# Seven-product pairs in the down projection: 30 of 44 instead of 24, with activation sums kept in DRAM and weights tiled by the host

## The chip, the cores and the metric

The kernel runs on one core of one Trainium2 chip. The metric is the device time of one execution, in microseconds; the median of several runs is given. TensorE (PE) multiplies, PEld is its weight load, VectorE (DVE), ScalarE (ACT) and GpSimd (POOL) do the elementwise work, and SyncE (SP) issues nearly all transfers.

## The reference

The input is one sequence of 256 tokens with 2048 features, in float32. What is computed, cut to what matters here:

```python
hn  = rmsnorm(h, mix_norm_pre);  proj = hn @ w_in            # 2048 x 3616
mix = concat(ssd_mixer(z, xbc, dt), pool_mixer(u)) @ w_out   # 2048 x 2048
h   = h + rmsnorm(mix, mix_norm_post)
hn  = rmsnorm(h, ffn_norm_pre)
up  = hn @ w_ffn_up                                          # 2048 x 11264
gate, val = split(up)                                        # 5632 each
gate = dwconv_centred(gate, conv_w, conv_b)                  # three taps over tokens
h   = h + rmsnorm((gelu(gate) * val) @ w_ffn_down, ffn_norm_post)  # 5632 x 2048
g   = sigmoid(rmsnorm(h, ple_norm_pre) @ w_ple_gate)         # 2048 x 2048
h   = h + rmsnorm(g * (p @ w_ple), ple_norm_post)
```

## The kernel before

**Precision.** Every float32 operand of a large product is split into a high part (a rounded copy by ScalarE) and a low part (the rest, a subtraction by VectorE). A product of two operands then takes three matmuls: high by high, high by low, low by high. For weights, `split` does this (L141 to L153: the copy on L152, the subtraction on L153); the parts lie in tiles of the tags `whi` and `wlo`, with five buffers each. All matmuls go through the helper `mm` on L87.

**Stages, in order.** The input projection and the mixers, w_out, then the gated MLP in two stages: "up" (11 slices of 512 features, first the gate columns, then the value columns) and "down" (two halves of 1024 output columns). Last come the gate of the per-layer embedding (also two halves) and the output. The names of tiles begin with `ug` and `uv` in up, `dn0` and `dn1` in the two halves of down, `gt0` and `gt1` in the gate, and `wo` in w_out.

**Pairs.** `token_major` (L291) walks a half in pairs: two blocks of 128 input features by 1024 columns of weights, loaded as one tile of the tag `raw` (three buffers, L156). Down has 22 pairs a half and the gate 8. A plain pair takes 24 matmuls of 512 columns.

**Seven products.** `seven_products` (L239) does a pair by Strassen's scheme: the two blocks of 128 rows and the two of 512 columns form a 2 x 2 block product, made with seven block products instead of eight, 21 matmuls. It needs sums of the four weight blocks (`add_blocks`, L235 to L237: one addition of 1024 columns and two of 512) and sums of the four activation blocks (`pair_sums`, L774: four small additions, L777 to L780, then the split in high and low on L781 and L782). The weights come as four split tiles: `a` (512 columns), `b`, `c` and `d` (1024 each); `c` and `d` are made of the sums. `combine` (L269) adds the seven results at the end of a half's last such pair. Pairs treated so are called fast.

**Where the sums come from.** If a pair is listed in `sums_`, its weight sums were made during up and the pair loads them (`t`) beside 0.75 MB of its weights; else the pair loads its 1 MB and `add_blocks` runs in place. The w_out stage works in the second way, as its pair `wo10` shows. Before, all 24 fast pairs of down (12 a half) and the 4 of the gate have their weight sums made during up: `block_sums` (L208) loads a pair, adds, and stores the result in DRAM (two stay on chip). These jobs lie in a list, `work`, of 88 entries; `aside` (L196) runs one entry behind each of the 88 units of up. The activation sums are made in down itself by `hid_sums` (L920): 20 times, as four of the first half's are kept on chip for the second (`dn_keep`).

**Activations in down.** `get_hid` (L899) splits two blocks of the hidden activations into one tile of the tag `hs` (two buffers; the copy on L903, the subtraction on L904). Small tiles of 1024 columns share the tag `mid` (three buffers).

**Order.** Each engine works through its own queue in program order; a scheduler puts the instructions into these queues ahead of time. `load` (L119) issues transfers on SP. `first_gate` (L943) is called at pair 16 of the second half: it prepares the first pair of the gate by two casts on ScalarE (L948, L950) and one accumulating transfer issued by GpSimd (L949). `back`, at pair 13, loads the residual again.

Of the kernel before, what the change touches and what calls it, by code (L numbers as in the profile page):

```python
# [16 lines left out]
P = 128  # L17
L = 256
# [33 lines left out]
def build(nc, a, out):  # L52
    x = a["x"][0]
    w_in, w_out, w_up = a["w_in"][0], a["w_out"][0], a["w_ffn_up"][0]
    w_down, w_gate, w_ple = a["w_ffn_down"][0], a["w_ple_gate"][0], a["w_ple"][0]
    out = out[0]

    with tile.TileContext(nc) as tc, \
# [37 lines left out]
        c_dt = DSSD + 1536  # L96
        r0 = wp.tile([P, 2048], F32, tag="raw", bufs=3, name="dtur0")
        for n in range(2):
            first = ins(nc.scalar.dma_start(r0[:, n * 352:(n + 1) * 352],
                                            w_in[:P, c_dt + n * 352:c_dt + (n + 1) * 352]))  # L100
# [55 lines left out]
        def raw(name, src, a_, b_):  # L156
            r = wp.tile([P, 2048], F32, tag="raw", bufs=3, name=name)
            if src is None:
                return r
            last["dma"] = load(r[:, :a_ * b_].rearrange("p (a b) -> p a b", a=a_), src, True)  # L160
            return r
# [46 lines left out]
        def block_sums(name, w, c0, k, held):  # L208


            pg = []

            def fetch():
                r = page(f"{name}b{c0}_{k}")
                pg.append(r)
                load(r.rearrange("p (k c) -> p k c", k=2),
                     w[k * P:(k + 2) * P, c0:c0 + 1024].rearrange("(k p) c -> p k c", p=P))
# [12 lines left out]
            return [fetch], [], [add], [store]  # L230
# [8 lines left out]
        def seven_products(name, stage, w, k0, c0, a_, acc, alt, start, stop):  # L239

            if (stage, c0, k0) in sums_:
                r = raw(f"{name}r", None, 0, 0)
                last["dma"] = load(r[:, 512:1536], w[(k0 + 1) * P:(k0 + 2) * P, c0:c0 + 1024], True)
                last["dma"] = load(r[:, :512], w[k0 * P:(k0 + 1) * P, c0:c0 + 512], True)
                t, held = sums_[stage, c0, k0]
                if not held:
                    t = page(f"{name}t")
                    last["dma"] = load(t, sums_[stage, c0, k0][0], True)  # L250
                b11 = split(f"{name}a", r[:, :512], 512)
                b2 = split(f"{name}b", r[:, 512:1536], 1024)
            else:
                r = t = raw(f"{name}r", w[k0 * P:(k0 + 2) * P, c0:c0 + 1024]
                            .rearrange("(k p) c -> p k c", p=P), 2, 1024)
# [35 lines left out]
        def token_major(name, w, c0, ks, get, acc, tail=1, fast=(), alt=None, sums=None, at=()):  # L291
# [3 lines left out]
            for u in range(nu):  # L295
# [3 lines left out]
                if u in fast:  # L299
                    if u == fast[0]:  # L300
# [3 lines left out]
                r = None if f"{name}{k0}_0" in ready else raw(f"{name}r{k0}", w[k0 * P:(k0 + 2) * P, c0:c0 + 1024]  # L304
                                                               .rearrange("(k p) c -> p k c", p=P), 2, 1024)
# [17 lines left out]
        def feature_major(name, w, c0, get, acc):  # L323

            for u in range(4):
                r = raw(f"{name}r{u}", w[u * 512:(u + 1) * 512, c0:c0 + 512]
                        .rearrange("(k p) c -> p k c", p=P), 4, 512)
# [12 lines left out]
        def feature_pairs(name, w, c0, get, acc):  # L340


            for u in range(2):
                r = raw(f"{name}r{u}", w[u * 1024:(u + 1) * 1024, c0:c0 + 256]
                        .rearrange("(k p) c -> p k c", p=P), 8, 256)
# [97 lines left out]
        for u in range(0, NK, 2):  # L443
            r = [wp.tile([P, 2048], F32, tag="raw", bufs=3, name=f"dtur{u}") if u else r0, page(f"dtur{u + 1}")]
            for j in range(2):
                k = u + j
                if k == 0:
                    last["dma"] = load(r[0][:, 704:1056], w_in[:P, c_dt + 704:c_dt + 1056])
                    xload(1, 2)
                    x_panel(1, 2)  # L450
                    continue
                for c0, c1 in ((0, 704), (704, 1056)) if k == 1 else ((0, 1056),):
                    last["dma"] = load(r[j][:, c0:c1], w_in[k * P:(k + 1) * P, c_dt + c0:c_dt + c1])
# [29 lines left out]
        with tc.issue_after(half[0]), tc.issue_after(half[1]):  # L483
# [11 lines left out]
            for a_ in range(4):  # L495
# [17 lines left out]
        load(pmat.rearrange("p (g s t) -> p g s t", g=4, s=2),  # L513
             a["pool_matrix"].rearrange("g (s p) t -> p g s t", p=P))
        poolw = page("poolw")
        load(poolw.rearrange("p (g c d) -> p g c d", g=4, c=2),
             a["pool_w"][0].rearrange("g (c p) d -> p g c d", p=P))
# [122 lines left out]
        def xbc(slab):  # L640
            acc = main(f"xbc{slab}")
            feature_major(f"xb{slab}", w_in, DSSD + slab * 512, hn, acc)
# [88 lines left out]
        token_major("z", w_in, 0, list(range(NK)), hn, zacc)  # L731
# [42 lines left out]
        def pair_sums(name, s, o, a11, a21, a12, a22):  # L774

            s1, s2, s3, s4 = (s[:, i * P:(i + 1) * P] for i in range(4))
# [5 lines left out]
            nc.vector.tensor_sub(o[:, 512:], s[:, :512], o[:, :512].bitcast(F32))  # L782
            return {f"s{i + 1}": (o[:, i * P:(i + 1) * P], o[:, 512 + i * P:512 + (i + 1) * P]) for i in range(4)}
# [89 lines left out]
        hid = []  # L873
        for s in range(DFF // 512):
            sc = mid(f"gr{s}")
            for i in range(2):
                ga = main(f"ga{s}{i}")
                feature_pairs(f"ug{s}{i}", w_up, s * 512 + i * 256, hf, ga)
# [8 lines left out]
            for i in range(2):  # L887
                va = main(f"va{s}{i}")
                feature_pairs(f"uv{s}{i}", w_up, DFF + s * 512 + i * 256, hf, va)
# [9 lines left out]
        def get_hid(k):  # L899
            if k % 2 == 0:  # L900
                t = lp.tile([P, 1024], F32R, tag="hs", bufs=2, name=f"hs{k}")
                src = hid[k // 8][:, (k % 8) * L:(k % 8 + 2) * L]
                nc.scalar.copy(t[:, :512], src)  # L903
                nc.vector.tensor_sub(t[:, 512:], src, t[:, :512].bitcast(F32))  # L904
# [13 lines left out]
        keep, kept = [], {}  # L918

        def hid_sums(k):  # L920


            (h1, l1), (h2, l2) = get_hid(k), get_hid(k + 1)
            if k not in kept:
                src = hid[k // 8][:, (k % 8) * L:(k % 8 + 2) * L]
# [17 lines left out]
        def first_gate():  # L943

            r, hi, lo = page("gtf"), page("gtfh", F32R), page("gtfl", F32R)
            src = w_gate[:2 * P, :1024].rearrange("(k p) c -> p k c", p=P)
            last["dma"] = load(r.rearrange("p (k c) -> p k c", k=2), src)
            nc.scalar.activation(lo, r, AF.Copy, scale=-1.0)  # L948
            nc.gpsimd.dma_start(lo.rearrange("p (k c) -> p k c", k=2), src, accum_op=ALU.add)  # L949
# [14 lines left out]
        vg = [page(f"vg{t}") for t in range(2)]  # L964
# [27 lines left out]
        for half in range(2):  # L992
# [12 lines left out]
            for t in range(2):  # L1005
                for n, (o, c0) in enumerate(columns(acc[t])):
# [15 lines left out]
                    else:  # L1022
                        nc.scalar.activation(so, sv, AF.Square, accum_out=q)
                    nc.vector.tensor_mul(vg[t][:, c], v, gple[:, c])
# [5 lines left out]
def laid_out(a):  # L1030

    def cols(*vs):
        return np.concatenate([v.reshape(-1, P).T for v in vs], axis=1)

    return {
        "x_cols": np.concatenate([cols(a["mix_norm_pre"][0]),
# [24 lines left out]
def constants():  # L1061
    return {"pool_matrix": pool_matrix()}
# [16 lines left out]
```

## Time and profile before

| | us |
|---|---|
| median of 3 runs | 1123.02 (1122.94 to 1123.16) |
| the profiled execution | 1123.11 |
| span of its instructions | 1121.3 |
| granted TensorE clock, mean | 0.997 |

| stage | window, us | PE busy | DVE busy | ACT busy |
|---|---|---|---|---|
| up | 311.2 to 789.0 | 477.80 | 386.76 | 240.31 |
| down, first half | 789.0 to 902.5 | 113.50 | 105.23 | 81.65 |
| down, second half | 902.5 to 1016.7 | 114.15 | 104.77 | 84.56 |
| gate, first part | 1016.7 to 1068.0 | 51.30 | 42.96 | 33.73 |

The profile comes from one execution, some 2 us longer than the span because it begins before the first instruction and ends behind the last. A row of a timeline gives start, duration, engine, line of the kernel, operation, and the tiles as output<-inputs; what stands in brackets is how long the engine was idle before it and what ended the wait. Durations of neighbours overlap a little, so a price is best read from start to start.

### The profile page before, as it was taken

To read this page: it belongs to the slowest core of one execution; us is meant where nothing else is said; L and a number is where in the kernel's file an instruction comes from. 1 tells how busy PE (TensorE), PEld (TensorE's weight loads), DVE (VectorE), ACT (ScalarE), POOL (GpSimd) and SP (SyncE) were. 2 spreads that over 40 slices of the span, in tenths; PEclk is the share of its full clock that TensorE was granted. 3 is DMA by queue.
4 is the path that set the end of the run, shared out by engine and by line. 5 is a ranking of instruction groups with operands and counts; after the bars stand their busy time and mean duration, and the time that the engine had idled before them with its cause. 6 is when DMAs were issued, how large, how long until landed. Compare 5 with 4: busy or idle time off the path is not lost.

```text
span 1121.3 us, 15775 instructions
## 1 busy us (share of the span) xinstructions
PE 1109.1 (99%) x5971; PEld 956.4 (85%) x5971; DVE 925.2 (83%) x1275; ACT 663.9 (59%) x927; POOL 76.2 (7%) x86
## 2 busy tenths in 40 slices
PE   9999999999999999999999999999999999999996
PEld 9999987888888888888888888888888888888875
DVE  6569895799898877877877768888899999889795
ACT  6847663555764554554545445445677777786672
POOL 0200004200110100000000000000000000001001
PEclk9999999999999999999999999999999999999998
DMA  9862447456789989989999898996969688995663
GB/s 363 310 207 96 170 161 269 151 188 190 252 308 347 328 300 336 314 289 309 333 330 314 276 330 289 325 304 224 339 185 334 221 286 301 383 318 177 230 235 109
DMA packets 145996, 300.87 MB, mean 268 GB/s; under 512 B 5504, under 2 KB 98560, under 8 KB 137856
## 3 DMA queue, kind: packets, MB, share of 16 engines
q1 hardware_dynamic: 145360, 298.45, 78.6%
q0 software_dynamic: 272, 1.05, 0.5%
q8 instruction: 47, 0.77, 0.3%
q10 hardware_dynamic: 288, 0.36, 0.1%
q14 instruction: 29, 0.24, 0.1%
HBM read 268.38 MB, written 31.46 MB: 267 GB/s over the span
## 4 chain that ended last, share of the span: by engine, by line
PE 96%; ACT 1%; DVE 1%; issue 1%; POOL 1%; POOLq 0%; DVEq 0%; ACTq 0%
PE va L87 22%; PE ga L87 21%; PE dna L87 14%; PE woa L87 7%; PE xbc L87 6%; PE gt L87 5%; PE dtu L87 4%; PE z L87 4%; PE dns L87 3%; PE dn0s L87 1%; PE dn1s L87 1%; PE ple L87 1%; PE pw L87 1%; PE yd L87 0%; PE gts L87 0%
## 5 line engine op out<-in xcount | busy, mean ns | idle before, releaser
L87 PE MATMUL ga<-wox,ug_0h 128*128 128x512 f32 x352 | 125.5, 395 | 0.0
L87 PE MATMUL ga<-wox,ug_1h 128*128 128x512 f32 x352 | 125.1, 394 | 0.0
L87 PE MATMUL va<-wox,uv_1h 128*128 128x512 f32 x352 | 124.8, 393 | 0.0
L87 PE MATMUL va<-wox,uv_0h 128*128 128x512 f32 x352 | 124.8, 393 | 0.0
L87 PE MATMUL ga<-wox,ug_1l 128*128 128x256 f32 x352 | 99.1, 282 | 0.0
L87 PE MATMUL ga<-wox,ug_0l 128*128 128x256 f32 x352 | 99.1, 282 | 0.0
L87 PE MATMUL va<-wox,uv_1l 128*128 128x256 f32 x352 | 99.1, 281 | 0.0
L87 PE MATMUL va<-wox,uv_0l 128*128 128x256 f32 x352 | 99.1, 281 | 0.0
L87 PEld LDWEIGHTS va<-wox,uv_1h 128*128 128x128 f32 x352 | 66.1, 188 | 15.0
L87 PEld LDWEIGHTS va<-wox,uv_0h 128*128 128x128 f32 x352 | 66.1, 188 | 15.0
L87 PEld LDWEIGHTS ga<-wox,ug_0h 128*128 128x128 f32 x352 | 66.1, 188 | 14.9
L87 PEld LDWEIGHTS ga<-wox,ug_1h 128*128 128x128 f32 x352 | 66.1, 188 | 14.9
L87 PEld LDWEIGHTS ga<-wox,ug_0l 128*128 128x128 f32 x352 | 66.2, 188 | 0.1
L87 PEld LDWEIGHTS ga<-wox,ug_1l 128*128 128x128 f32 x352 | 66.2, 188 | 0.0
L87 PEld LDWEIGHTS va<-wox,uv_0l 128*128 128x128 f32 x352 | 66.2, 188 | 0.0
L87 PEld LDWEIGHTS va<-wox,uv_1l 128*128 128x128 f32 x352 | 66.2, 188 | 0.0
L885 POOL TENSOR_TENSOR fc<-fc,rfb 128x1024 f32<-128x1024 f32 x11 | 28.0, 2547 | 438.6 <-ACT fc L884 438.6
L87 PE MATMUL dna<-dn_0h,hs 128*128 128x512 f32 x160 | 50.1, 393 | 0.0
L87 PE MATMUL dna<-dn_1h,hs 128*128 128x512 f32 x160 | 49.9, 393 | 0.0
L235 DVE TENSOR_TENSOR dnb<-dnb 128x1024 f32<-128x1024 f32 x24 | 30.8, 1283 | 17.8 <-DMA dnb<-w_ffn_down 17.6
L903 ACT CAST hs<-hid 128x512 fp32r<-128x512 f32 x44 | 27.2, 617 | 23.2 <-PE dna L87 14.8
L904 DVE TENSOR_TENSOR hs<-hid,hs 128x512 fp32r<-128x512 f32 x44 | 30.2, 686 | 9.8 <-ACT hs L903 9.7
(1903 smaller groups left out, 3105.3 us busy)
## 6 DMA issues: line engine op xcount, KB each, us to landing
dnb<-w_ffn_down SPq DMA_DIRECT2D x24, 1024.0 KB, 10.4
dns<-dnb SPq DMA_DIRECT2D x22, 1024.0 KB, 7.4
dn0r<-w_ffn_down SPq DMA_DIRECT2D x10, 1024.0 KB, 6.0
dn1r<-w_ffn_down SPq DMA_DIRECT2D x10, 1024.0 KB, 7.1
zr<-w_in SPq DMA_DIRECT2D x8, 1024.0 KB, 5.1
dtur<-w_in SPq DMA_DIRECT2D x14, 528.0 KB, 8.7
wo0r<-w_out SPq DMA_DIRECT2D x7, 1024.0 KB, 5.6
wo1r<-w_out SPq DMA_DIRECT2D x6, 1024.0 KB, 5.5
```

The costliest lines, as they stand in the source:

```text
L87: last["pe"] = ins(nc.tensor.matmul(o, lhsT, rhs, start=start, stop=stop, skip_group_check=True))
L235: nc.vector.tensor_add(v[:, 0:2], v[:, 0:2], v[:, 1::2])
L885: nc.gpsimd.tensor_tensor(cv.rearrange("p (f t) -> p f t", f=4), cv.rearrange("p (f t) -> p f t", f=4), rfb.unsqueeze(1).to_broadcast([P, ...
L903: nc.scalar.copy(t[:, :512], src)
L904: nc.vector.tensor_sub(t[:, 512:], src, t[:, :512].bitcast(F32))
```

## The change

- **More fast pairs.** Down goes from 12 and 12 fast pairs to 16 and 14 of 22, the gate from 4 to 5 of 16. The order of the gate's second half is changed to suit.
- **Weight sums.** Eleven of down's 30 fast pairs (`dn_own`) have no weight sums made during up: they run `add_blocks` in place. The other 19 and the gate's 5 are still made during up, spaced 7/2 entries apart instead of 3.
- **Activation sums.** The sums of 16 pairs are made during up, in a tile of the tag `hs`, and stored in DRAM by SP. Down fetches them for each of its 30 fast pairs by a transfer of 512 KB issued by GpSimd, into a `mid` tile.
- **Layout.** The host lays all weights out in tiles, so that each load is contiguous: 8 KB for each partition, where rows of 1 KB (up), 2 KB (xbc) or 4 KB were gathered before.
- The two result pages of the last stage are allocated later.

```diff
-        dn_fast, gt_fast, dn_keep = ((2, 3, 5, 7, 8, 10, 12, 13, 15, 16, 18, 19), (2, 3, 5, 7, 8, 10, 12, 13, 15, 16, 18, 19)), ((4, 6), (1, 2)), (3, 8, 13, 18)
-        gt_ks = list(range(NK)), [0, 1, 12, 13, 8, 9, 2, 3, 4, 5, 6, 7, 10, 11, 14, 15]
-        which = [("dn", w_down, c * 1024, 2 * u) for c in range(2) for u in dn_fast[c]] + \
+        dn_fast, gt_fast = ((2, 3, 4, 5, 6, 8, 9, 10, 11, 12, 14, 15, 16, 17, 18, 19), (2, 3, 4, 5, 8, 9, 10, 11, 12, 14, 15, 17, 18, 19)), ((4, 5, 6), (1, 2))
+        dn_own = (5, 9, 11, 15, 17), (4, 8, 10, 12, 15, 17)
+        gt_ks = list(range(NK)), [0, 1, 8, 9, 10, 11, 2, 3, 4, 5, 6, 7, 12, 13, 14, 15]
+        which = [("dn", w_down, c * 1024, 2 * u) for c in range(2) for u in dn_fast[c] if u not in dn_own[c]] + \
             [("gt", w_gate, c * 1024, gt_ks[c][2 * u]) for c in range(2) for u in gt_fast[c]]
...
-                work[3 * i + 2 + j].extend(jobs)
+                work[7 * i // 2 + 2 + j].extend(jobs)
...
+        def hid_sums_jobs(k):
+            o = []
+            def make():
+                o.append(lp.tile([P, 1024], F32R, tag="hs", bufs=2, name=f"he{k}"))
+                pair_sums(f"he{k}", o[0][:, 512:].bitcast(F32), o[0],
+                          *(hid_part(k)[:, i * P:(i + 1) * P] for i in range(4)))
+            def store():
+                kept[k] = dp.tile([P, 1024], F32, tag=f"hsum{k}", bufs=1, name=f"hsum{k}")
+                load(kept[k], o[0].bitcast(F32))
+            return [make], [store]
+        for u in sorted({*dn_fast[0], *dn_fast[1]}):
+            for j, jobs in enumerate(hid_sums_jobs(2 * u)):
+                work[u // 2 * 8 + u % 2 * 2 + 6 + j].extend(jobs)
...
         def hid_sums(k):
+            o = mid(f"hd{k}", F32R)
+            nc.gpsimd.dma_start(o.bitcast(F32), kept[k])
             (h1, l1), (h2, l2) = get_hid(k), get_hid(k + 1)
-            if k not in kept:
-                src = hid[k // 8][:, (k % 8) * L:(k % 8 + 2) * L]
-                n = dn_keep.index(k // 2) if k // 2 in dn_keep else -1
-                if n >= 0 and n % 2 == 0:
-                    keep.append(page(f"hsum{k}", F32R))
-                o = keep[-1][:, n % 2 * 1024:(n % 2 + 1) * 1024] if n >= 0 else mid(f"he{k}", F32R)
-                d = pair_sums(f"hd{k}", mid(f"hd{k}"), o, *(src[:, i * P:(i + 1) * P] for i in range(4)))
-                if n >= 0:
-                    kept[k] = d
-            else:
-                d = kept[k]
-            return dict(d, a11=(h1[:, :P], l1[:, :P]), a12=(h2[:, :P], l2[:, :P]), a22=(h2[:, P:], l2[:, P:]))
+            return dict(sums_in(o), a11=(h1[:, :P], l1[:, :P]), a12=(h2[:, :P], l2[:, :P]), a22=(h2[:, P:], l2[:, P:]))
...
+    def tiles(w, nk, nc):
+        k, c = w.shape
+        return w.reshape(k // P // nk, nk, P, c // nc, nc).transpose(3, 0, 2, 1, 4).reshape(c // nc, k // P // nk, P, nk * nc)
...
+        "w_up": tiles(a["w_ffn_up"][0], 8, 256).reshape(2, DFF // 512, 2, 2, P, 2048),
+        "w_down": tiles(a["w_ffn_down"][0], 2, 1024),
+        "w_gate": tiles(a["w_ple_gate"][0], 2, 1024),
```

More of the change, by code (lines that the diff above doesn't have):

```diff
@@ L53, in build @@
     x = a["x"][0]
-    w_in, w_out, w_up = a["w_in"][0], a["w_out"][0], a["w_ffn_up"][0]
-    w_down, w_gate, w_ple = a["w_ffn_down"][0], a["w_ple_gate"][0], a["w_ple"][0]
+    w_dtu, w_xbc, w_z, w_out, w_up = a["w_dtu"], a["w_xbc"], a["w_z"], a["w_out_"], a["w_up"]
+    w_down, w_gate, w_ple = a["w_down"], a["w_gate"], a["w_ple_"]
     out = out[0]
@@ L154, in split, with raw @@
             return hi, lo
-        def raw(name, src, a_, b_):
+        def raw(name, src=None):
             r = wp.tile([P, 2048], F32, tag="raw", bufs=3, name=name)
-            if src is None:
-                return r
-            last["dma"] = load(r[:, :a_ * b_].rearrange("p (a b) -> p a b", a=a_), src, True)
+            if src is not None:
+                last["dma"] = load(r, src, True)
             return r
@@ L243, in seven_products @@
             if (stage, c0, k0) in sums_:
-                r = raw(f"{name}r", None, 0, 0)
-                last["dma"] = load(r[:, 512:1536], w[(k0 + 1) * P:(k0 + 2) * P, c0:c0 + 1024], True)
-                last["dma"] = load(r[:, :512], w[k0 * P:(k0 + 1) * P, c0:c0 + 512], True)
+                r = raw(f"{name}r")
+                last["dma"] = load(r[:, 512:1536], w[c0 // 1024, k0 // 2][:, 1024:], True)
+                last["dma"] = load(r[:, :512], w[c0 // 1024, k0 // 2][:, :512], True)
                 t, held = sums_[stage, c0, k0]
@@ L447, in build @@
                 if k == 0:
-                    last["dma"] = load(r[0][:, 704:1056], w_in[:P, c_dt + 704:c_dt + 1056])
+                    last["dma"] = load(r[0][:, 704:1056], w_dtu[0][:, 704:1056])
                     xload(1, 2)
@@ L452, in build @@
                 for c0, c1 in ((0, 704), (704, 1056)) if k == 1 else ((0, 1056),):
-                    last["dma"] = load(r[j][:, c0:c1], w_in[k * P:(k + 1) * P, c_dt + c0:c_dt + c1])
+                    last["dma"] = load(r[j][:, c0:c1], w_dtu[k][:, c0:c1])
                 if k == 1:
@@ L730, in build @@
         zacc = [main(f"z{t}") for t in range(2)]
-        token_major("z", w_in, 0, list(range(NK)), hn, zacc)
+        token_major("z", w_z, 0, list(range(NK)), hn, zacc)
         assert not work
@@ L945, in first_gate @@
             r, hi, lo = page("gtf"), page("gtfh", F32R), page("gtfl", F32R)
-            src = w_gate[:2 * P, :1024].rearrange("(k p) c -> p k c", p=P)
-            last["dma"] = load(r.rearrange("p (k c) -> p k c", k=2), src)
+            last["dma"] = load(r, w_gate[0, 0])
             nc.scalar.activation(lo, r, AF.Copy, scale=-1.0)
-            nc.gpsimd.dma_start(lo.rearrange("p (k c) -> p k c", k=2), src, accum_op=ALU.add)
+            nc.gpsimd.dma_start(lo, w_gate[0, 0], accum_op=ALU.add)
             nc.scalar.copy(hi, r)
@@ L963, in build @@
         gple = gload("gple", a["ple_norm_post"][0])
-        vg = [page(f"vg{t}") for t in range(2)]
+        vg = []
         sq = [[], []]
@@ L1023, in build @@
                         nc.scalar.activation(so, sv, AF.Square, accum_out=q)
+                    if half == n == 0:
+                        vg.append(page(f"vg{t}"))
                     nc.vector.tensor_mul(vg[t][:, c], v, gple[:, c])
@@ L1068 @@
     arrays.update({n: np.ascontiguousarray(v) for n, v in laid_out(arrays).items()})
-    arrays.update(constants())
+    arrays.update({n: np.ascontiguousarray(v) for n, v in constants().items()})
     for n in ("p", "mix_norm_pre", "ssd_conv_w", "ssd_conv_b", "ssd_norm", "pool_scale", "ffn_norm_pre",
-              "ffn_conv_w", "ple_norm_pre", "ffn_conv_b", "ssd_dt_bias", "ssd_a_log", "ssd_d"):
+              "ffn_conv_w", "ple_norm_pre", "ffn_conv_b", "ssd_dt_bias", "ssd_a_log", "ssd_d", "w_in", "w_out",
+              "w_ffn_up", "w_ffn_down", "w_ple_gate", "w_ple", "pool_w"):
         del arrays[n]
```

56 lines of the change are left out of this document (28 added, 28 removed).

## The prediction

> **What bounds the kernel now.** I read the engine table and the shares of the chain of waits first.
>
> ```profile
> PE 1109.1 (99%) x5971; PEld 956.4 (85%) x5971; DVE 925.2 (83%) x1275; ACT 663.9 (59%) x927; POOL 76.2 (7%) x86
> ...
> PE 96%; ACT 1%; DVE 1%; issue 1%; POOL 1%; POOLq 0%; DVEq 0%; ACTq 0%
> ```
>
> TensorE is busy for 1109.1 of the span's 1121.3 us. Fewer products are worth their full time as long as nothing new makes PE wait. Next come the stages that the change touches (up, the two halves of down, the first part of the gate): us, then the busy time of PE, PEld, DVE, ACT and POOL, the granted clock, the DMA engines' share, GB/s.
>
> ```profile
> 311.20:789.00 477.80, 477.80 (x2739) 419.38 (x2738) 386.76 (x491) 240.31 (x318) 28.01 (x11) 1.00 0.93 308
> 789.00:902.50 113.50, 113.50 (x493) 92.25 (x492) 105.23 (x146) 81.65 (x108) 0.00 (x0) 1.00 0.77 261
> 902.50:1016.70 114.20, 114.15 (x495) 92.36 (x494) 104.77 (x143) 84.56 (x109) 3.78 (x8) 1.00 0.91 323
> 1016.70:1068.00 51.30, 51.30 (x240) 41.74 (x239) 42.96 (x64) 33.73 (x51) 4.61 (x10) 1.00 0.66 215
> ```
>
> PE never waits in up and down, and its clock is full. VectorE comes close behind it: 210.0 of the 227.7 us of down. It makes every low part that PE multiplies, so in down the question is whether VectorE keeps its lead.
>
> **What PE saves.** The chain in order of time (start, us, what) gives the price of a product of 512 columns.
>
> ```profile
> 820.11 5.55 PE dna L87 x24
> ...
> 891.49 11.05 PE dna L87 x48
> ```
>
> A plain pair is 24 products, 5.55 us: 0.2313 each. A pair by seven products has 21, 4.86 us. Down gets six more such pairs (24 to 30) and the gate one (4 to 5): 7 x 3 x 0.2313 = 4.86 us less. The two instruction lists agree, with 21 matmul rows fewer. That the change does not do this is excluded.
>
> **What VectorE must do for a pair.** Its timeline (start, us) around pairs 4 and 5 of the first half:
>
> ```profile
> 806.38 1.22 DVE L153 TENSOR_TENSOR dn_0l<-dn0r,dn_0h 128x1024 fp32r<-128x1024 f32 x1
> 807.51 1.22 DVE L153 TENSOR_TENSOR dn_1l<-dn0r,dn_1h 128x1024 fp32r<-128x1024 f32 x1
> 808.65 0.68 DVE L153 TENSOR_TENSOR dn010al<-dn010r,dn010ah 128x512 fp32r<-128x512 f32 x1
> 809.25 0.68 DVE L782 TENSOR_TENSOR he<-hd,he 128x512 fp32r<-128x512 f32 x1
> 809.85 1.22 DVE L153 TENSOR_TENSOR dn010bl<-dn010r,dn010bh 128x1024 fp32r<-128x1024 f32 x1
> ...
> 812.72 0.28 DVE L777 TENSOR_TENSOR hd<-hid 128x128 f32<-128x128 f32 x1
> ...
> 813.65 1.22 DVE L153 TENSOR_TENSOR dn010dl<-dn010t,dn010dh 128x1024 fp32r<-128x1024 f32 x1
> ```
>
> From start to start, 1024 columns take 1.13 to 1.14 us, 512 take 0.60, and the four small sums from 812.72 to 813.65 take 0.93. A plain pair (P) needs two wide subtractions and the activations' low part: 2.87 us, which is 2.68 less than PE's 5.55. A seven-product pair whose sums are all ready (L) needs 0.60 + 3 x 1.135 + 0.60 = 4.61, 0.25 less than PE's 4.86. With its activation sums made in place, as 20 of the 24 pairs are now, it needs 0.93 + 0.60 more: 6.14, 1.28 over. So today's fast pairs spend lead and plain pairs restore it.
>
> The change takes these 1.53 us away (20 x 1.53 = 30.6 us). In exchange 11 of the 30 pairs ("own", O: 5, 9, 11, 15, 17 and 4, 8, 10, 12, 15, 17) must add their weight blocks in place. No such pair runs in down now, but the w_out stage has one:
>
> ```profile
> 258.89 0.68 DVE L153 TENSOR_TENSOR wo10al<-wo10r,wo10ah 128x512 fp32r<-128x512 f32 x1
> 259.88 1.23 DVE L153 TENSOR_TENSOR wo10bl<-wo10r,wo10bh 128x1024 fp32r<-128x1024 f32 x1 [0.30 <-ACT wo10bh L152]
> 261.02 0.68 DVE L782 TENSOR_TENSOR csp<-css,csp 128x512 fp32r<-128x512 f32 x1
> 261.62 1.22 DVE L235 TENSOR_TENSOR wo10r<-wo10r 128x1024 f32<-128x1024 f32 x1
> 262.87 0.69 DVE L236 TENSOR_TENSOR wo10r<-wo10r 128x512 f32<-128x512 f32 x1
> 263.60 0.69 DVE L237 TENSOR_TENSOR wo10r<-wo10r 128x512 f32<-128x512 f32 x1
> 264.21 1.22 DVE L153 TENSOR_TENSOR wo10cl<-wo10r,wo10ch 128x1024 fp32r<-128x1024 f32 x1
> 265.49 1.23 DVE L153 TENSOR_TENSOR wo10dl<-wo10r,wo10dh 128x1024 fp32r<-128x1024 f32 x1
> ...
> 264.40 1.06 ACT L152 CAST wo10dh<-wo10r 128x1024 fp32r<-128x1024 f32 x1 [0.40 <-DVE wo10r L237]
> ```
>
> The last row is ScalarE's: it cannot copy the sums before VectorE's last add, and VectorE then waits for the copy. The eight rows take 258.89 to 265.49, plus 1.13: 7.73 us (the 512-wide L782 stands for the low part of the activations). That is 2.87 over PE's 4.86. Lower bound: 4.61 + 1.14 + 2 x 0.60 = 6.95 (2.09 over), if every ScalarE round trip is hidden. Upper bound: one more wait for a 1.06 us copy, 8.8 us (3.94 over). I take 7.73: the changed VectorE order has the same form, adds between the b and the c subtraction, c and d behind them. On ScalarE the next pair's copies are queued behind those of c and d, so they come late too.
>
> Over down, before makes 20 x 2.87 + 24 x 4.61 + 20 x 1.53 = 198.6 us of this work and after, at 6.95, 14 x 2.87 + 19 x 4.61 + 11 x 6.95 = 204.3. So 210.0 + 5.7 = 215.7 us stand against 223.5 of PE, and the round trips (11 x 0.78) fill what is left.
>
> **How much lead there is.**
>
> ```profile
> 824.01 1.22 DVE L153 TENSOR_TENSOR dn014dl<-dn014t,dn014dh 128x1024 fp32r<-128x1024 f32 x1
> ...
> 830.26 1.23 DVE L153 TENSOR_TENSOR dn016dl<-dn016t,dn016dh 128x1024 fp32r<-128x1024 f32 x1
> ...
> 829.20 0.39 PE L87 MATMUL dna<-dn014dl,hs 128*128 128x512 f32 x1
> ...
> 834.07 0.40 PE L87 MATMUL dna<-dn016dl,hs 128*128 128x512 f32 x1
> ...
> 829.17 1.05 ACT L152 CAST dn016dh<-dn016t 128x1024 fp32r<-128x1024 f32 x1 [0.33 <-PE dn0s L87]
> ```
>
> The last low part of a fast pair behind a plain one is ready 829.20 - 825.23 = 3.97 us before PE uses it; of a fast pair behind a fast one 834.07 - 831.49 = 2.58. The copy at 829.17 waits for PE to give a buffer back (five of each kind), so I take 3.97 and 2.58 as caps.
>
> Now the walk; a negative lead is a PE stall and restarts from zero. First half: 2 to 4 are L, capped at 2.58; 5 O stalls 0.29; 6 L 0.25; 7 P 2.93; 8 L 3.18; 9 O 0.31; 10 L 0.56; 11 O stalls 2.31; 12 L, 13 P, 14 L 3.18; 15 O 0.31; 16 L 0.56; 17 O stalls 2.31; 18, 19 L 0.50. Sum 4.9. Second half: 2, 3 L 2.58; 4 O stalls 0.29; 5 L, 6 P 2.93; 7 P 3.97 (cap); 8 O 1.10; 9 L 1.35; 10 O stalls 1.52; 11 L 0.25; 12 O stalls 2.62; 13 P, 14 L 2.93; 15 O 0.06; 16 P 2.74; 17 O stalls 0.13. Sum 4.6. Together 9.5.
>
> **Smaller terms.**
>
> ```profile
> 896.89 0.68 DVE L904 TENSOR_TENSOR hs<-hid,hs 128x512 fp32r<-128x512 f32 x1
> ...
> 982.66 0.69 DVE L904 TENSOR_TENSOR hs<-hid,hs 128x512 fp32r<-128x512 f32 x1 [2.89 <-ACT hs L903]
> ```
>
> Behind each half's last fast pair VectorE also combines the seven results. Its low part at 896.89 to 897.57 already comes as PE turns to the last pair, at 891.49 + 5.55 = 897.04. With a lead of 0.50 there, I add 1.0 a half (0 to 2.1): 2.0. In the second half VectorE waited 2.89 us behind ScalarE's casts for the gate; lead covers that now, and I add 1.0 (0 to 2.9). In up, 16 activation sums come in (24.5 us) and four block sums go out:
>
> ```profile
> L235 DVE TENSOR_TENSOR dnb<-dnb 128x1024 f32<-128x1024 f32 x24 | 30.8, 1283 | 17.8 <-DMA dnb<-w_ffn_down 17.6
> ```
>
> 4 x (1.28 + 2 x 0.69) = 10.6. So VectorE has 386.8 + 13.9 = 401 of 477.8 us in up and PE covers it. On SP's queue 16 stores of 512 KB come in; each waits for its sum, with up's weight loads behind it, and four loads and four stores of 1 MB go out. Three tiles loaded ahead cover such a wait (PE has none in up); without that cover it would be a copy and a subtraction, under 2 us a time. I add 0.3 for up and gate (0 to 1).
>
> **The transfers.**
>
> ```profile
> GB/s 407 300 364 361 225 150 175 187 227 352 368 275 310 336 249 191 184 184 310 65 332 402 281 349 298 291 330 376 231 412 418 414 290 369 287 284 416 307 263 119
> DMA packets 16045, 66.56 MB, mean 292 GB/s; under 512 B 1457, under 2 KB 1457, under 8 KB 12993
> ...
> gtfl<-w_ple_gate POOLq DMA_DIRECT2D x1, 1024.0 KB, 14.4
> ```
>
> Down moves 66.56 MB now. Its weights are 24 x 1.75 + 20 - 2 = 60 MiB now (two sums stay on chip) and 17 x 1.75 + 2 x 0.75 + 11 + 14 = 56.25 after; 30 fetched activation sums add 15: 78.4 MB over 223.5 us, 351 GB/s. DMA is busy for 0.77 x 113.5 + 0.91 x 114.2 = 191 us, so it moves 348 GB/s while busy, and slices reach 412 to 418 (the queue is often empty). Rows grow from 4 to 8 KB, so I count no stall; at 348 it would be 225 us, 1.5 more than PE. A sum is asked for about three fast pairs (some 14 us) ahead, and half a megabyte should land in half of 14.4 us.
>
> The sums are fetched through GpSimd, and the trace shows that engine and VectorE in each other's way:
>
> ```profile
> 774.61 2.41 POOL L885 TENSOR_TENSOR fc<-fc,rfb 128x1024 f32<-128x1024 f32 x1 [40.71 <-ACT fc L884]
> ...
> 775.00 2.56 DVE L782 TENSOR_TENSOR he<-hd,he 128x512 fp32r<-128x512 f32 x1 [0.51 <-ACT he L781]
> ...
> 980.63 1.43 POOL L949 DMA_DIRECT2D gtfl<-w_ple_gate  x1 [203.62 <-ACT gtfl L948]
> ```
>
> Beside GpSimd's multiplication a 0.68 us subtraction took 2.56. A DMA issue holds GpSimd for 1.43 us; the only one in down fell where VectorE was idle (979.8 to 982.7), so their meeting is not shown. Bounds: 0 to 30 x 1.43 = 43 us of VectorE time. I take 0, as an issue reads no tile.
>
> The Trainium skill ("SBUF — State Buffer", "SBUF: two separate sides") warns that descriptors of GpSimd's DMAs are not written while VectorE runs a two-port mode, and advises SP's or ScalarE's queue. It names for that mode a single-source f32 copy, and VectorE's work in down is two-source; by it the loads would not be late, and no run here shows it yet. The sum is the same by the page.
>
> **Sum.** Against the profiled execution's 1123.11 us (median of the runs 1123.02, as good as equal): 1123.11 - 4.86 + 9.5 + 2.0 + 1.0 + 0.3 = 1131.0 us.
>
> **Rivals.**
>
> (1) *The adds spread* (faster). They need only the loaded tile and no split buffer, so VectorE may run them in the time that the caps leave idle (7.8 us over down). For: VectorE idles for 17.7 us in down now. Against: the order places them in the pair itself. Decides where an own pair's c and d come at least 2.9 us early: 1123.11 - 4.86 = 1118.3.
>
> (2) *Round trips hidden* (no change). With 6.95 the same walk stalls 1.0 and 1.8 us; with half of the tails, 1.0, and 0.3: 1122.3. For: ScalarE idles for over a quarter of down. Against: the 0.40 and 0.30 us waits in the own pair above.
>
> (3) *The fetches hurt* (slower still). Sums queued behind the gate's 14.4 us load, descriptor writing that holds VectorE in ten of 30 issues (10 x 0.3 to 0.9), or DMA at 348 GB/s: 3 to 9 us over the forecast, 1134 to 1140. With 8.8 for an own pair the walk stalls about 22 us: 1143.
>
> **How the numbers follow.** Forecast with its own range of 1126 to 1136: 0.58. Rival 1: 0.17. Rival 2: 0.10. Rival 3: 0.15. A measurement tells 0.2%, 2.25 us, from no change. So faster 0.17, same 0.10, slower 0.73. The range, 1119 to 1140, leaves out most of rival 1 and the upper end of rival 3.
>
> **What would show it.** Right: PE about 4.9 us less busy; waits of PE on VectorE or ScalarE at the c and d parts of own pairs, 11 and 17 of the first half, 10 and 12 of the second; VectorE near 97% over down, and down about 235 us instead of 227.7. Wrong: down near 223 us with no PE wait (rival 1), or PE and ScalarE waiting for the fetched sums (rival 3), or waits in up.

## The result and the profile after

The change makes the kernel slower: 1138.07 us median (1137.37 to 1139.1, 4 runs) against 1123.09 before. The ratio is 1.0132, 95% interval 1.012 to 1.0145. The profiled execution took 1137.37 us with a span of 1135.4, 14.1 more than before's.

The engine table and the chain's shares:

```profile
PE 1112.0 (98%) x5950; PEld 949.6 (84%) x5950; DVE 948.3 (84%) x1296; ACT 671.7 (59%) x938; POOL 98.6 (9%) x116
...
PE 82%; DVE 9%; ACT 3%; DMA 3%; issue 2%; POOL 1%; SPq 0%; DVEq 0%; POOLq 0%; ACTq 0%
```

There are 21 matmuls fewer, yet TensorE's share of the chain fell from 96% to 82%, and VectorE, ScalarE and transfers now stand in it. The stages again (us, busy time of PE, PEld, DVE, ACT, POOL, clock, DMA share, GB/s); the windows are up, the two halves of down, and the first part of the gate:

```profile
311.20:789.00 477.80, 477.80 (x2740) 419.39 (x2740) 395.82 (x545) 247.80 (x331) 35.49 (x13) 1.00 0.85 313
789.00:909.90 120.90, 114.94 (x482) 88.95 (x481) 108.42 (x122) 80.85 (x104) 9.23 (x17) 1.00 0.81 296
909.90:1031.60 121.70, 116.58 (x489) 90.20 (x488) 111.37 (x126) 82.98 (x107) 9.97 (x17) 1.00 0.87 330
1031.60:1083.00 51.40, 51.40 (x240) 41.88 (x239) 48.08 (x74) 37.58 (x56) 4.16 (x12) 1.00 0.67 243
```

Up takes its old 477.8 us. The halves of down take 120.9 and 121.7, where 16 x 4.86 + 6 x 5.55 = 111.1 and 14 x 4.86 + 8 x 5.55 = 112.4 would do. Some 19 us are lost in down, at full clock. Beside 1.2 us behind the combination of the results, PE's longest waits there are (us in total, times, longest):

```profile
PE dns L88 <- ACT dn034ch L151: 0.7, 1, 0.7
PE dns L88 <- ACT dn124ch L151: 0.7, 1, 0.7
PE dns L88 <- ACT dn022ch L151: 0.7, 1, 0.7
PE dna L88 <- ACT dn130dh L151: 0.6, 1, 0.6
PE dna L88 <- ACT dn022dh L151: 0.5, 1, 0.5
PE dna L88 <- ACT dn120dh L151: 0.5, 1, 0.5
PE dna L88 <- ACT dn034dh L151: 0.5, 1, 0.5
```

All are for the c or d parts of own pairs: 11 (dn022) and 17 (dn034) of the first half, 10, 12 and 15 (dn120, dn124, dn130) of the second. This is VectorE's timeline for pair 11, from its first subtraction to that of pair 12, with ScalarE's copy of d and PE's first matmuls on c and d behind it:

```profile
844.89 0.68 DVE L152 TENSOR_TENSOR dn022al<-dn022r,dn022ah 128x512 fp32r<-128x512 f32 x1
845.49 1.22 DVE L152 TENSOR_TENSOR dn022bl<-dn022r,dn022bh 128x1024 fp32r<-128x1024 f32 x1
846.62 1.22 DVE L232 TENSOR_TENSOR dn022r<-dn022r 128x1024 f32<-128x1024 f32 x1
847.76 0.68 DVE L922 TENSOR_TENSOR hs<-hid,hs 128x512 fp32r<-128x512 f32 x1
848.36 0.68 DVE L233 TENSOR_TENSOR dn022r<-dn022r 128x512 f32<-128x512 f32 x1
849.01 1.23 DVE L152 TENSOR_TENSOR dn022cl<-dn022r,dn022ch 128x1024 fp32r<-128x1024 f32 x1
850.15 0.69 DVE L234 TENSOR_TENSOR dn022r<-dn022r 128x512 f32<-128x512 f32 x1
852.00 1.23 DVE L152 TENSOR_TENSOR dn022dl<-dn022r,dn022dh 128x1024 fp32r<-128x1024 f32 x1 [1.17 <-ACT dn022dh L151]
853.15 0.69 DVE L152 TENSOR_TENSOR dn024al<-dn024r,dn024ah 128x512 fp32r<-128x512 f32 x1
...
850.93 1.05 ACT L151 CAST dn022dh<-dn022r 128x1024 fp32r<-128x1024 f32 x1 [1.95 <-DVE dn022r L234]
...
847.92 0.40 PE L88 MATMUL dna<-dn022bh,hd 128*128 128x512 f32 x1
849.03 0.50 PE L88 MATMUL dns<-dn022ch,hd 128*128 128x512 f32 x1 [0.71 <-ACT dn022ch L151]
...
852.03 0.50 PE L88 MATMUL dna<-dn022dh,hs 128*128 128x512 f32 x1 [0.55 <-ACT dn022dh L151]
```

The pair takes 853.15 - 844.89 = 8.26 us of VectorE. Its last addition (850.15) stands right ahead of the d subtraction, with nothing between them; ScalarE can copy d only then, and VectorE idles for 1.17 us. Read in the same way, the eleven own pairs form two groups. In eight the last addition stands behind the c subtraction, as here: 9, 11, 15 and 17 of the first half take 8.48, 8.26, 8.48 and 8.26, and 8, 10, 12 and 15 of the second take 8.49, 8.26, 8.26 and 8.89 (in the last the gate's casts come between). In three, 5 of the first half and 4 and 17 of the second, all additions stand ahead of c; they take 7.20, 7.20 and 7.81. This is the end of pair 5, whose first subtraction began at 811.46:

```profile
815.66 0.68 DVE L234 TENSOR_TENSOR dn010r<-dn010r 128x512 f32<-128x512 f32 x1
816.26 1.22 DVE L152 TENSOR_TENSOR dn010cl<-dn010r,dn010ch 128x1024 fp32r<-128x1024 f32 x1
817.52 1.23 DVE L152 TENSOR_TENSOR dn010dl<-dn010r,dn010dh 128x1024 fp32r<-128x1024 f32 x1
818.66 0.69 DVE L152 TENSOR_TENSOR dn012al<-dn012r,dn012ah 128x512 fp32r<-128x512 f32 x1
```

### The profile page after: what moved, and what is told of

Read it like the earlier page. It is cut to its first block, busy times and chain, and to the rows that moved or that the text cites. A ratio compares the mean times of both kernels' runs of the same rounds, so it can differ in the third digit from the quotient of the medians.

```text
span 1135.4 us, 15843 instructions
## 1 busy us (share of the span) xinstructions
PE 1112.0 (98%) x5950; PEld 949.6 (84%) x5950; DVE 948.3 (84%) x1296; ACT 671.7 (59%) x938; POOL 98.6 (9%) x116
## 4 chain that ended last, share of the span: by engine, by line
PE 82%; DVE 9%; ACT 3%; DMA 3%; issue 2%; POOL 1%; SPq 0%; DVEq 0%; POOLq 0%; ACTq 0%
PE va L88 22%; PE ga L88 21%; PE woa L88 7%; PE xbc L88 6%; PE dna L88 5%; PE gt L88 5%; PE dtu L88 4%; PE z L88 4%; PE dns L88 1%; PE ple L88 1%; DVE hs L922 1%; PE dn0s L88 1%; DMA dn136r<-w_down 1%; DMA gtf<-w_gate 1%; DMA dn116r<-w_down 1%
## 5 line engine op out<-in xcount | busy, mean ns | idle before, releaser
L904 POOL TENSOR_TENSOR fc<-fc,rfb 128x1024 f32<-128x1024 f32 x11 | 34.2, 3105 | 393.5 <-ACT fc L903 393.4
L88 PE MATMUL dna<-dn_0h,hs 128*128 128x512 f32 x112 | 37.1, 399 | 1.6 <-DVE dna L285 1.2
L939 POOL DMA_DIRECT2D hd<-hsum x30 | 16.8, 560 | 234.8 <-PE dn0s L88 81.5
L421 DVE SCALAR_TENSOR_TENSOR fc<-gr,vt,fc 128x255 f32<-128x255 f32 x88 | 36.7, 478 | 0.0
```

The source lines that it names most:

```text
L88: last["pe"] = ins(nc.tensor.matmul(o, lhsT, rhs, start=start, stop=stop, skip_group_check=True))
L421: nc.vector.scalar_tensor_tensor(o[:, lo:hi], i[:, lo + d:hi + d], vec(wcol + j * wstep + f), o[:, lo:hi], op0=ALU.mult, op1=ALU.add)
L904: nc.gpsimd.tensor_tensor(cv.rearrange("p (f t) -> p f t", f=4), cv.rearrange("p (f t) -> p f t", f=4), rfb.unsqueeze(1).to_broadcast([P, ...
L939: nc.gpsimd.dma_start(o.bitcast(F32), kept[k])
```

## The experiments

All times are medians; before, on the same chip, was 1123.2 to 1123.4. Start times of pairs are read from PE's timeline, from the first matmul of one pair to that of the next. The edits are cut to the lines that matter, and long tuples are written short.

**No own pairs.** Is it the own pairs, the fetches through GpSimd, or the transfers? The eleven own pairs become plain ones.

```diff
-        dn_fast = ((2, 3, 4, 5, 6, 8, 9, 10, 11, 12, 14, ...), (2, 3, 4, 5, 8, 9, 10, ...))
+        dn_fast = ((2, 3, 4, 6, 8, 10, 12, 14, 16, 18, 19), (2, 3, 5, 9, 11, 14, 18, 19))
-        dn_own = (5, 9, 11, 15, 17), (4, 8, 10, 12, 15, 17)
+        dn_own = (), ()
```

> The 11 own pairs of down become plain pairs; everything else stays (19 fast pairs with premade sums, 19 fetched activation sums through GpSimd, tiled weights, 5 fast pairs in the gate). Theory, own pairs: VectorE's extra work and its wait for ScalarE in them are what stops PE, so the 16.8 us of stalls at own pairs go and 11 x 0.69 = 7.6 us of PE work come back: 1138.1 - 16.8 + 7.6 = about 1129, 1126 if the tails shorten too, and no wait of PE on VectorE or ScalarE inside down's fast pairs. Rival, GpSimd's fetches: 19 of 30 remain, so about 19/30 of the 19 us stays: 1123.1 + 2.8 + 12 = 1138. Rival, transfers: down moves 5.8 MB less of 75.9, so most of the stalls stay: 1134 or more.

1126.36 us, ratio 1.0029 (1.0018 to 1.004). PE has no wait in down:

```profile
789.10:903.40 114.30, 114.30 (x497) 92.99 (x496) 89.13 (x98) 74.89 (x96) 6.51 (x12) 1.00 0.78 294
903.40:1019.90 116.50, 116.50 (x505) 94.59 (x504) 87.20 (x95) 74.52 (x93) 6.13 (x12) 1.00 0.84 315
```

With 33 matmuls more than the change it is 11.7 us faster. Nineteen fetches through GpSimd cost nothing here. With the own pairs go their additions, eleven fetches and 5.6 of 75.9 MB; the next two runs part these. Of the 3.2 us over before, 2.8 are the price of five fewer fast pairs in down, less one more in the gate (4 x 0.69).

**The order inside an own pair.** Same pairs and transfers; the additions write to a tile of their own, so that none waits for a split, and they are issued first.

```diff
-                r = t = raw(f"{name}r", w[c0 // 1024, k0 // 2])
+                r = raw(f"{name}r", w[c0 // 1024, k0 // 2])
+                t = page(f"{name}t")
+                add_blocks(r, t)        # t = sums of r's blocks; was in place, behind the b split
```

> The own pairs write their block sums to a tile of their own, as the other fast pairs have, and the additions are issued ahead of the splits, so none of them waits for a split and ScalarE's copies of c and d find them ready. Same work, same transfers, same 30 fast pairs. Theory, own pairs' round trip: a pair costs VectorE 6.95 instead of the 8.3 to 8.5 us that it takes now, the walk with 6.95 stalls 2.8 us, and with 2 us of tails the time is 1123.1 - 4.9 + 2.8 + 2.1 = about 1123 (1120 to 1126). If it is only the quantity of VectorE's work and not the order: no change, 1136 to 1138. Rival, GpSimd's fetches or transfers: no change, 1138.

1128.92 us, ratio 1.0051 (1.0036 to 1.0066): 9.2 us of the 15 come back with the quantity of VectorE's work unchanged. Its timeline for the same pair 11, whose 1024-wide addition ran two pairs earlier:

```profile
844.18 0.68 DVE L234 TENSOR_TENSOR dn022t<-dn022r,dn022t 128x512 f32<-128x512 f32 x1
844.78 0.69 DVE L152 TENSOR_TENSOR dn022al<-dn022r,dn022ah 128x512 fp32r<-128x512 f32 x1
845.38 0.68 DVE L235 TENSOR_TENSOR dn022t<-dn022r,dn022t 128x512 f32<-128x512 f32 x1
845.98 1.22 DVE L152 TENSOR_TENSOR dn022bl<-dn022r,dn022bh 128x1024 fp32r<-128x1024 f32 x1
847.12 1.22 DVE L152 TENSOR_TENSOR dn022cl<-dn022t,dn022ch 128x1024 fp32r<-128x1024 f32 x1
848.25 1.22 DVE L152 TENSOR_TENSOR dn022dl<-dn022t,dn022dh 128x1024 fp32r<-128x1024 f32 x1
849.39 0.68 DVE L924 TENSOR_TENSOR hs<-hid,hs 128x512 fp32r<-128x512 f32 x1
849.99 0.69 DVE L152 TENSOR_TENSOR dn024al<-dn024r,dn024ah 128x512 fp32r<-128x512 f32 x1
```

849.99 - 844.18 + 1.14 = 6.95 us, with no wait in these rows: the prediction's lower bound. The time is still 6 us over the 1123 expected. By starts, down loses some 11 us beyond its products, where the change loses some 19. Two pieces are plain. The early addition of pair 11 had itself waited for its load, and PE lost 0.8 us at pair 9, whose subtractions stood behind it. In the second half, at pair 14, VectorE waited for a copy, and ScalarE for premade sums on their way (PE lost 1.6 us). The rest is not traced to its causes.

```profile
834.41 1.23 DVE L233 TENSOR_TENSOR dn022t<-dn022r 128x1024 f32<-128x1024 f32 x1 [1.78 <-DMA dn022r<-w_down]
...
978.49 1.23 DVE L152 TENSOR_TENSOR dn128cl<-dn128t,dn128ch 128x1024 fp32r<-128x1024 f32 x1 [4.24 <-ACT dn128ch L151]
...
977.41 1.05 ACT L151 CAST dn128ch<-dn128t 128x1024 fp32r<-128x1024 f32 x1 [5.63 <-DMA dn128t<-dns]
```

**The queue of the fetches.**

```diff
-            nc.gpsimd.dma_start(o.bitcast(F32), kept[k])
+            load(o.bitcast(F32), kept[k], True)      # SP
```

> The activation sums are fetched by SP's queue instead of GpSimd's; nothing else changes. Theory, own pairs: 1138 within 2 us (or some us slower, since a fetch that waits for its tile now holds the weight loads behind it on SP). Rival, GpSimd's fetches hold VectorE or land late: the 19 us of stalls shrink, 1119 to 1130.

1137.95 us, ratio 1.0131 (1.0116 to 1.0147): the same as the change. The fetches land sooner by SP (5.2 us median in down against 7.9 by GpSimd), and that is worth nothing. GpSimd's part is not in the loss.

**The layout alone**, with everything else as before (the later result pages with it).

```diff
-                load(r.rearrange("p (k c) -> p k c", k=2),
-                     w[k * P:(k + 2) * P, c0:c0 + 1024].rearrange("(k p) c -> p k c", p=P))
+                load(r, w[c0 // 1024, k // 2])          # and so for every weight
```

> The weights tiled by the host and the later result pages alone; fast pairs, premade weight sums and activation sums as before. Theory, own pairs: no part of the loss; PE waited for no transfer before, so 1123 within 2 us. Rival, layout (longer rows compete with other traffic, or land later): some of the 15 us, 1126 or more. A gain would show at the opening or in the gate, 1 to 2 us at most.

1123.42 us, ratio 1.0 (0.999 to 1.0009). The DMA engines are busy for less of up at the same 308 GB/s, and PE, which never waited for them, gains nothing:

```profile
311.20:789.00 477.80, 477.80 (x2740) 419.68 (x2740) 387.21 (x491) 240.37 (x317) 28.83 (x11) 1.00 0.82 308
```

**All weight sums made in up.**

```diff
-        dn_own = (5, 9, 11, 15, 17), (4, 8, 10, 12, 15, 17)
+        dn_own = (), ()
-                work[7 * i // 2 + 2 + j].extend(jobs)
+                work[12 * i // 5 + 2 + j].extend(jobs)
```

> All 35 pairs have their weight sums made during up (the jobs spaced 12/5 entries apart instead of 7/2); no own pairs, the same 30 + 5 fast pairs. Theory, own pairs: VectorE's stalls in down go; up gets 11 x 2.66 = 29 us more of VectorE (396 + 29 of 478) and 23 MB more of transfers (150 + 23 MB, at 369 GB/s while busy 469 of 478 us). 1123.1 - 4.9 + 2 = about 1120 if up still hides it. Rival, transfers: down now needs 75.9 + 8.7 MB, 227 us at the 372 GB/s that it moves while busy, against 223 of PE: 1125 to 1135, with PE or ScalarE waiting for loads of weights.

1178.25 us, ratio 1.049 (1.0475 to 1.0506). Neither number was right: down begins at 836.4 instead of 789.0, so up loses 47 us. In up, what SP waited for, and then PE's waits:

```profile
SPq L118 <- DVE he L774: 145.1, 16, 11.4
...
PE ga L88 <- ACT ug_0h L151: 14.0, 8, 5.0
PE ga L88 <- DVE ug_0l L152: 10.0, 10, 1.9
```

SP stood for 145 us behind VectorE's sums (L774; 61.9 us in the change), with the weight loads behind those stores. The DMA engines were not full in up (shares of 0.83 to 0.87). PE's idle time in up is 30 of the 47 us, and its granted clock there was 0.98 instead of 1.00. How much of the 47 us is SP's order was not tried with this many sums. The 11 sums cannot simply be moved back to up as the stores stand.

**24 sums in up, none own, and who stores the activation sums.** Before's fast pairs with the fetched activation sums; then the same with the stores of these issued by GpSimd.

```diff
+        dn_fast[0] = dn_fast[1] = (2, 3, 5, 7, 8, 10, 12, 13, 15, 16, 18, 19);  dn_own = (), ()
+                work[20 * i // 7 + 2 + j].extend(jobs)
                                                    # second run, in store():
-                load(kept[k], o[0].bitcast(F32))
+                nc.gpsimd.dma_start(kept[k], o[0].bitcast(F32))
```

> Before's 12 + 12 fast pairs, all with weight sums made during up (29 with the gate's 5, 20/7 entries apart), no own pairs; activation sums of 12 pairs from DRAM as in the change. PE does 3 matmuls less than before. If up still hides VectorE's and SP's extra jobs: 1123.1 - 0.7 = 1122.4 (1121.5 to 1124). If up begins to fail between 24 and 35 premade sums, as it did by 47 us with 35: 1125 to 1145, with PE waiting for the ug and uv tiles in up.

> The run with 24 premade sums and no own pairs, with the activation sums' 12 stores in up issued by GpSimd instead of SP. In that run SP waited 95.7 us in up for VectorE's sums with weight loads behind it, and down began 3.8 us later than in the change. If SP's order is what makes up late: down begins near 789.0 again and the time falls from 1132.1 to about 1128. If it is VectorE's or the DMA engines' mere load: no change.

1132.1 us with SP's stores, 1128.8 with GpSimd's (ratios 1.0077 and 1.0051, each within 0.0015). PE's first matmul of down, with SP's and then with GpSimd's stores:

```profile
792.79 0.62 PE L88 MATMUL dna<-dn_0h,hs 128*128 128x512 f32 x2
...
789.57 0.62 PE L88 MATMUL dna<-dn_0h,hs 128*128 128x512 f32 x2
```

The late start of down goes, as the order of SP's queue would have it. Little of what is left is in up (0.8 us). PE's longest wait in the second run is in the second half of down, where VectorE has time to spare (92.0 of 116.3 us) and the DMA engines have not (below the wait, what ScalarE waited for):

```profile
PE dns L88 <- ACT dn132ch L151: 2.8, 1, 2.8
...
989.60 1.04 ACT L151 CAST dn132ch<-dn132t 128x1024 fp32r<-128x1024 f32 x1 [3.85 <-DMA dn132t<-dns]
...
905.00:1021.30 116.30, 113.05 (x486) 90.62 (x485) 92.01 (x101) 78.70 (x97) 8.04 (x16) 1.00 0.93 356
```

A second half with 12 premade and 12 fetched sums beside the residual and the gate's first 2 MB asks for more than lands in time.

**Six own pairs between plain ones.** The 24 of the last run, with SP's stores, and pairs 4, 9 and 14 of each half as own pairs with a tile of their own.

```diff
+        dn_fast[0] = dn_fast[1] = (2, 3, 4, 5, 7, 8, 9, 10, 12, 13, 14, 15, 16, 18, 19)
+        dn_own = (4, 9, 14), (4, 9, 14)
```

> As the run with 24 premade sums, with three more fast pairs in each half (4, 9, 14), each between plain pairs or behind one, as own pairs whose block sums go to a tile of their own ahead of the splits: 30 fast pairs again. At 6.95 us a pair the walk has no stall (lowest lead 0.49), so the 15 + 3 matmuls come off in full: 1123.1 - 4.9 = 1118.3, 1121 with the tails and the gate's casts. If the price of an own pair were not the order but its mere work, each would cost near 1 us: 1124 to 1126. If up fails with 29 premade sums, it fails here too, 3 to 20 us more.

1140.86 us, ratio 1.0154 (1.0139 to 1.017). A miss: up loses 9 us (down begins at 798.3), and down takes 14 us more than its products. The second half's DMA share is 0.93 again. In the first half an addition, now ahead in VectorE's queue, waited for its load and held the pair before it:

```profile
862.54 1.23 DVE L233 TENSOR_TENSOR dn028t<-dn028r 128x1024 f32<-128x1024 f32 x1 [3.58 <-DMA dn028r<-w_down]
```

Pair 13 then took 6.73 us of PE instead of 4.86. Putting the additions first trades a wait for ScalarE for a possible wait for a load.

**Five own pairs.** The change's premade sums; only 5, 9, 15 and 8, 10 stay own, with sums in a tile of their own, and the other six are plain.

```diff
+        dn_fast = ((2, 3, 4, 5, 6, 8, 9, 10, 12, 14, 15, 16, 18, 19), (2, 3, 5, 8, 9, 10, 11, 14, 18, 19))
+        dn_own = (5, 9, 15), (8, 10)
```

> The premade sums of the change (19 + 5), five own pairs with sums in a tile of their own (5, 9, 15 and 8, 10); the six others plain. Against the run without own pairs 15 matmuls less: 1126.4 - 3.5 = 1122.9, to 1125 with what stalls are left at 9 and 10 and in the tails.

1124.51 us, ratio 1.0009 (1.0 to 1.0019). The first half has no stall. The second loses 1.8 us at pairs 14 and 15, where ScalarE waits for the gate's first load.

**Without the gate's early load**, on the version with the additions first (1128.92).

```diff
-                      fast=dn_fast, sums=hid_sums, at={13: back, 16: first_gate})
+                      fast=dn_fast, sums=hid_sums, at={13: back})
```

> As the run with the own pairs' sums in a tile of their own (1128.9), without the early preparation of the gate's first pair in down (2 MB of loads and two wide casts on ScalarE); the gate loads that pair as any other. If these are what still delays the second half's loads (dn128t came 4 us late there): 3 to 5 us of its stalls go, the gate's first pair may come up to 3 us late, 1125 to 1128. If VectorE's work alone makes the rest: 1129 or slower.

1132.01 us, ratio 1.0073 (1.0056 to 1.0089). That is slower than expected. Down ends 3.7 us earlier (1020.5 against 1024.2; 2.3 of it in the second half), as expected, but the gate loses more than that: PE waits 4.4 us for its `gt_1` parts. So these loads are a part of the second half's trouble, and worth their price.

**Mixed halves.** Two attempts at a version faster than before, both with the activation sums' stores by GpSimd. The first: 15 fast pairs in the first half (own 4, 9, 14), 10 in the second (own 8, 10). The other: the same first half, and a second half as before, 12 fast pairs whose activation sums VectorE makes in down.

```diff
+        dn_fast[0] = (2, 3, 4, 5, 7, 8, 9, 10, 12, 13, 14, 15, 16, 18, 19);  dn_own = (4, 9, 14), (8, 10)
+        dn_fast[1] = (2, 3, 5, 8, 9, 10, 11, 14, 18, 19)
                                                    # the other:
+        dn_fast[1] = (2, 3, 5, 7, 8, 10, 12, 13, 15, 16, 18, 19);  dn_own = (4, 9, 14), ()
+            if len(calls) > len(dn_fast[0]):    # calls: the pairs so far; true in the second half
+                o = mid(f"he{k}", F32R)
+                pair_sums(f"hd{k}", mid(f"hd{k}"), o, *(hid_part(k)[:, i * P:(i + 1) * P] for i in range(4)))
```

> First half of 15 fast pairs (12 premade, own 4, 9, 14 with sums in a tile of their own), second half of 10 (8 premade, own 8, 10), 25 premade sums with the gate's, stores of activation sums by GpSimd. PE has 18 matmuls less than before (6 x 0.69 = 4.2 us, counted with the gate's one and down's one): 25 against 24 pairs in down and 5 against 4 in the gate are 2 x 0.69 = 1.4 us: 1121.7 without any stall, 1122.5 to 1124 with 1 to 2 us in the second half, where the gate's first load comes in. If up fails at 25 premade sums: 1125 or more.

> What the runs point to, put together: the first half with 15 fast pairs and fetched activation sums (12 premade weight sums, own 4, 9, 14 with sums in a tile of their own); the second half as before, 12 fast pairs whose activation sums VectorE makes in down, so that nothing more is loaded there; 5 fast pairs in the gate, 29 premade sums, stores of activation sums by GpSimd, tiled weights. PE has 4 x 3 matmuls less than before: 1123.1 - 2.8 = 1120.3, and with 0.5 to 1 us in up and up to 1 us in the second half 1121 to 1122.5. If the second half's stalls of the earlier runs were VectorE's and not the transfers': 1124 or more.

1125.35 (ratio 1.0021, 1.0011 to 1.003) and 1123.26 us (ratio 0.9999, 0.999 to 1.0008). The first came out as expected if up fails: down begins 1.5 us late, and the second half loses 2.4 us behind pair 14. The second is 0.8 us slower than the 1121 to 1122.5 expected. It has no listed wait of PE in the second half (by starts it loses 0.7 us at pair 16, where before loses 0.3), and 12 matmuls less than before; of the 2.8 us that they save 2.2 go at pairs 13 and 14 of the first half (6.69 and 5.18 us of PE instead of 4.86), where VectorE waits 3.5 us for `dn028r` as above. No version beat before.

## Why the prediction was right, and where its sizes were off

Direction and mechanism hold. The loss is in the predicted place, and two runs show the cause: without own pairs 11.7 us come back, and with the same work in another order 9.2. The forecast of 1131.0 was 7 us short: 1138.07 lies outside the forecast's own range of 1126 to 1136, in the 1134 to 1140 that was given to rival 3, whose causes the runs rule out. By its own steps:

- **PE's saving.** 21 matmuls fewer, and fast pairs without a stall take 4.82 to 4.86 us: held.
- **The price of an own pair.** This term was mis-sized. The 7.73 us came from `wo10`, where the c subtraction stands between the last addition and the d subtraction and hides part of ScalarE's copy. The prediction gave all eleven pairs this order. Three have it, and take 7.20 to 7.81. In the other eight the last addition follows c, the copy is not hidden, and the pair takes 8.26 to 8.49 (8.89 with the gate's casts), near the upper bound of 8.8.
- **The walk.** Lost time in us, measured from pair to pair:

| own pair | 5 | 9 | 11 | 15 | 17 | sum | 4 | 8 | 10 | 12 | 15 | 17 | sum |
|---|---|---|---|---|---|---|---|---|---|---|---|---|---|
| predicted | 0.29 | 0 | 2.31 | 0 | 2.31 | 4.9 | 0.29 | 0 | 1.52 | 2.62 | 0 | 0.13 | 4.6 |
| measured | 0.4 | 1.2 | 3.1 | 1.1 | 3.1 | 9.0 | 0.4 | 0 | 2.4 | 3.1 | 1.5 | 0.6 | 7.9 |

  The pattern is right: the worst are the own pairs two places behind another one. The sum is 17.0 instead of 9.5. With each pair's own price the same walk gives 6.9 and 7.3, together 14.3: the prices account for some 4.8 of the missing 7.5 us. The other 2.7 stand mainly at 5, 9 and 15 of the first half and 4 of the second, where this walk sees 0 to 0.4 lost; why they lose more is open. The second half's 15 has the gate's casts in it, which the prediction counted apart (1.0).
- **Smaller terms.** The turns of the halves cost 0.9 and 1.0, against 1.0 each: held. Up gave 0.2, and the gate and the end no more than their matmuls less would have it, against 0.3 for both: held. The gate's casts are in the walk's 17.0. Together: -4.9 + 17.0 + 1.9 + 0.2 = 14.2, against 14.1 between the spans. So what the forecast lacked is all in the walk.
- **Rival 1, the adds spread:** false in the change; VectorE's order kept them inside the pair. In the run with the additions first they did spread, and the 1118.3 was not reached. **Rival 2, round trips hidden:** false for the change, but 6.95 is real in the other order; its 1122.3 was not reached there (1128.9), where late loads cost a part of the difference.
- **Rival 3, GpSimd's fetches:** false. An issue takes 0.54 us of GpSimd (one took 0.86, right behind the accumulating transfer's), not the 1.43 of the accumulating transfer before, and VectorE's subtraction beside it is not stretched (the row of 834.94; other ones take 1.22):

```profile
835.64 0.54 POOL L939 DMA_DIRECT2D hd<-hsum  x1 [9.86 <-PE dn0s L88]
...
834.94 1.23 DVE L152 TENSOR_TENSOR dn018cl<-dn018r,dn018ch 128x1024 fp32r<-128x1024 f32 x1
```

  The Trainium skill ("SBUF — State Buffer", "SBUF: two separate sides") ties the starving of GpSimd's descriptors to VectorE's two-port modes; the trace agrees in that two-source subtractions and these issues go side by side, and the swap of queues changed nothing (1137.95).
- **Transfers.** Down moved 75.93 MB in 242.6 us (78.4 in 223.5 were counted). With VectorE lengthening down, they were all but hidden: PE waited 0.2 us for the copy of a late load. They are the next bound: where VectorE had time, the second half stalled at a DMA share of 0.93.
- **Up.** "PE covers it" was right for 24 premade sums with 16 stores: SP stood for 61.9 us behind the activation sums, and PE did not feel it. With 29 sums and 12 stores up lost 4.0 us; 3.2 of them went when GpSimd issued the stores, so it was SP's order and not VectorE's share. With 35 up lost 47, and there SP's part is argued, not shown.
- **What would show it.** Waits at c and d of the pairs named, down longer: right. "PE about 4.9 us less busy" was wrong, as told below. Down came to 242.6 us, not 235, with VectorE busy for 219.8 of them: 91%, not 97%.

## What to carry to other kernels

When work moves to the engine that comes second, compare its time per step with the bottleneck's and walk the lead through the sequence: an average share of 96% hides single steps that cost 3 us more than they have. Price a step by a row with the same order of instructions, not only the same instructions: in eight of eleven pairs one addition stood behind a subtraction instead of ahead of it and uncovered a copy of 1 us, and issuing all additions first gave 9 us back. Every place from which the work can be taken has a limit of its own (here VectorE in down, SP's queue in up, the DMA engines in the second half), so look for the next limit before the work goes there.

## What the runs showed of the hardware

PE's busy time rose by 2.9 us, with 21 matmuls less. A matmul is listed with 0.39 us but the next starts 0.23 later, so a stall must first use up that overlap, and the first matmul behind a wait is listed with 0.50: between 847.92 and 849.03 above PE lost 0.88 us, of which the profile calls 0.71 a wait. The stalls of down sum to 19 us by starts and to 11 by PE's idle time. Lost time is read from starts.

Tiled weights raised what the DMA engines move while busy in up from 308 / 0.93 = 331 to 308 / 0.82 = 376 GB/s, for the same bytes (packets mostly under 2 KB before, 8 KB after), and the kernel's time did not move.
